# An fp32 hybrid encoder layer on one core: the lower half's x asked for together, the gate rows loaded into a sweep tile, and attention's pool and first product re-ordered

## The chip, the cores and the metric

The kernel runs on one core of one Trainium2 chip. The metric is the device time of one execution in microseconds; several executions are run and their median is given. One execution is also recorded by the hardware profiler, and everything said below of single instructions, waits and transfers comes from that record. The engines are PE (TensorE: matmuls, with PEld loading the stationary operand), DVE (VectorE), ACT (ScalarE), POOL (GpSimd) and SP (SyncE, which here only issues DMAs). "ACTq" and "SPq" are the instructions with which ACT and SP issue a DMA.

## The reference

One encoder layer in fp32, 2048 tokens by 1024 channels, batch 1. Cut to its skeleton:

```python
u = _rms_norm(h, norm_mix_g[l])
proj = u @ w_in[l]
hy = _short_conv_centred(proj[..., :HY_COLS], hy_conv_w[l], hy_conv_b[l])
y_hy = _group_rms_norm(_hyena(hy, spec, hy_skip[l]), hy_norm_g[l], HYENA_GROUPS)
qk = jax.nn.silu(_short_conv_centred(proj[..., HY_COLS:off], ml_conv_w[l], ml_conv_b[l]))
y_ml = _mlstm_bidirectional(q, k, v, o, gates, ml_gate_b[l])
y_ml = _group_rms_norm(y_ml, ml_norm_g[l], MLSTM_HEADS)
h = h + jnp.concatenate([y_hy, y_ml], -1) @ w_out[l]
h = h + _cross_attention(_rms_norm(h, norm_x_g[l]), _rms_norm(mem, norm_mem_g[l]), wq, wk, wv, wo)
h = h + jnp.square(jax.nn.relu(_rms_norm(h, norm_ff_g[l]) @ ff_w1[l])) @ ff_w2[l]
return _rms_norm(h, final_norm_g)
```

The hyena is a long convolution of order two (two gated stages over all 2048 tokens, through a Fourier transform), the mLSTM is a gated linear recurrence in two directions over 4 heads of 128 channels, and the cross-attention looks at 256 memory tokens.

## The kernel before

**Arithmetic.** A full-precision product of two fp32 operands is made of three fp32r matmuls (`mm3`, lines 357, 360, 361): each operand is split by ACT into a rounded high part (a cast, L368) and by DVE into the rest (a subtraction, L368), and high x high, high x low and low x high are added in PSUM. The products of the memory projection (L679, L696, L708) use plain fp32 operands.

**Stages**, in the order in which `program` (L2019) weaves them:

1. The input projection, with x transposed: channels on partitions, tokens along the row. Only one half of the tokens (1024) fits on the chip at a time as `xh`/`xl`, so the projection runs over the upper half, then the lower (`hf` = 1, then 0). `sweep` makes columns that need the short convolution; `natural` makes v, o and gate columns with tokens on partitions, in tiles of 128 tokens x 256 or 272 columns (8 x 3 matmuls each), and ACT copies each tile out of PSUM (L859) and issues its store (`od<-st`, L860).
2. While the rest of the projection runs, the hyena's first and second stages (`hyena`) are woven in; they read and write `fs`, `zs`, `zg` and `hy` in DRAM through SP's and ACT's queues.
3. `memproj` (L664): eight heads' worth of keys and values of the memory, folded with `wq` and `wo`. Each product's result is copied to a small tile by ACT (`kt`, L681; `o`, L686), and ACT issues the store (`gd<-o`, L698; `vw<-o`, L710). The hyena's last stage and the first pieces of `mlstm` run beside it.
4. `attention` (L1381) over four blocks of 512 tokens, woven with the remaining chunks of `mlstm`: the mixed rows are turned by PE (L1423), multiplied by `w_out`, the residual is added, and scores, softmax and values follow.
5. The feed-forward stage (`ffn`), from about 1800 us to the end, a two-level recursive block product.

**What sets the order.** Python generators yield rough costs and `weave` interleaves two of them by those costs; a scheduler then orders the instructions of each engine by a simulated timeline, within the dependences. Each engine runs its own list strictly in order. Tiles come from pools with a tag and a number of buffers; a new tile of a tag waits until the oldest holder of that tag is read out. A pool that opens where another has closed waits in the same way for the last users of the addresses. Each DMA, on SP's queue or ACT's, also counts on one of eight semaphore lanes, and before it is issued waits for the previous DMA of its lane; so a store that ACT issues can be held by a load that SP issued long before.

**The x of a half.** `prep_x` (L639) chains two `x_chunk`s (L524) of four steps. A step takes a tile of 128 x 2 x 512 (512 KB) from DRAM by `x_load` (L517), scales its two halves by gain and by the rows' inverse norm on DVE (L510), casts it on ACT and subtracts on DVE (L368), and so fills a quarter of `xh`/`xl`. The tiles have the tag `xn` with two buffers, so a load goes out only when the step before last has been read. For the lower half this begins at step `t == 4` of the last tile row of `natural(1, (3, 0, 1, 2), ...)`; the products that need it follow directly in `natural(0, (3,))`. The sweeps use big tiles `P` and `cv` (128 x 1088, two each), which lie empty between the upper half's last sweep and the lower half's first.

**The gate rows.** `mlstm` (L1189) first loads the packed gate rows (`rows`, 8 DMAs of 32 x 512, 64 KB each, L1218) into two tiles of its own pool. For every chunk of 128 tokens `loads` spreads rows of these over 128 partitions on DVE (L1240), POOL adds a mask (L1256) and multiplies by q (L1255), ACT takes exponentials (L1258), DVE multiplies with the scores (L1259). After that a chunk's body is 16 matmuls with v and the state (L1287, L1289), then the normalisation (L1292 to L1303), and a state update (`update`, L1150: scaling by ACT, L1156, matmuls L1162, DVE L1168 into `cf`). A chunk loads q, k, v, the gate o, k again and the backward state: `qn`, `kk_t`, `va`, `og`, `kn`, `cbn`, about 256 KB each. Chunks 0 and 1 are loaded and chunk 0 is scored ahead of the loop. `take(m, 6)` runs six steps of `mlstm` beside `memproj`.

**The opening of attention.** `tail_open` (L1331) opens the pool T; its tags `wn` (4 staging tiles), `act` (4 tiles), `wh`/`wl` and `acc` get their addresses in the order in which they are first used. `mixed(0)` loads four tiles of the hyena's rows `yh`, turns them (L1423) and yields; then `stream` loads the first columns of `w_out`, and the first product is made in two halves: for its two column tiles the k range 0 to 3 (the hyena's half), which needs only `yh`, and then, when the mLSTM's rows `ym` of the first 512 tokens are there (`next(mix)`), the range 4 to 7.

## Time and profile before

| | |
|---|---|
| median of 3 executions | 3120.02 us (3117.74 to 3126.49) |
| the profiled execution, its own time | 3121.71 us |
| its span, from the first instruction to the last | 3120.0 us |
| its mean granted TensorE clock | 0.988 |
| DMA traffic | 607 MB, 195 GB/s on the mean |

A window row gives, for each engine, busy time and the number of instructions in a stretch, then the TensorE clock granted as a share of full speed, the share of the 16 DMA engines' time that was busy (summed over overlapping packets, so it can pass 1), and GB/s. In a row of waits, "A <- B: total, times, longest" says that A stood idle because of B. In a row of the timeline, the start and length of a group of instructions come first, and what stands in brackets is the idle time of the engine just before it and what ended it.

### The profile page before, as it was taken

To read this page: it belongs to the slowest core of one execution; us is meant where nothing else is said; L and a number is where in the kernel's file an instruction comes from. 1 tells how busy PE (TensorE), PEld (TensorE's weight loads), DVE (VectorE), ACT (ScalarE), POOL (GpSimd) and SP (SyncE) were. 2 spreads that over 40 slices of the span, in tenths; PEclk is the share of its full clock that TensorE was granted. 3 is DMA by queue.
4 is the path that set the end of the run, shared out by engine and by line. 5 is a ranking of instruction groups with operands and counts; after the bars stand their busy time and mean duration, and the time that the engine had idled before them with its cause. 6 is when DMAs were issued, how large, how long until landed. Compare 5 with 4: busy or idle time off the path is not lost.

```text
span 3120.0 us, 42912 instructions
## 1 busy us (share of the span) xinstructions
PE 3025.7 (97%) x14257; PEld 2374.8 (76%) x14257; DVE 1957.9 (63%) x3428; ACT 1498.4 (48%) x2930; POOL 1145.9 (37%) x802
## 2 busy tenths in 40 slices
PE   8999999989999898999999999999999999999998
PEld 6655667766677666888888888887888888888876
DVE  7865465446747356777665656657555686565696
ACT  6543465533646225555544455556455443333335
POOL 0122011200223243233142337766455475242693
PEclk9999999999999998999999999999999999999999
DMA  6554767676877996455375657656644565353434
GB/s 212 189 197 163 231 211 219 177 237 199 252 209 241 277 321 228 140 197 179 130 268 191 212 168 240 202 180 227 202 152 151 169 216 183 112 166 113 161 92 172
DMA packets 444102, 607.07 MB, mean 195 GB/s; under 512 B 38494, under 2 KB 248542, under 8 KB 442856
## 3 DMA queue, kind: packets, MB, share of 16 engines
q1 hardware_dynamic: 405988, 546.54, 54.3%
q10 hardware_dynamic: 37892, 57.79, 5.4%
q8 instruction: 113, 1.85, 0.2%
q14 instruction: 109, 0.89, 0.1%
HBM read 401.79 MB, written 202.41 MB: 194 GB/s over the span
## 4 chain that ended last, share of the span: by engine, by line
PE 55%; DVE 2%; issue 1%; DMA 1%; ACT 0%; POOL 0%; SPq 0%; ACTq 0%; POOLq 0%; DVEq 0%
PE mm L357 12%; PE mm L360 12%; PE mm L361 12%; PE hy L361 6%; PE hy L357 6%; PE hy L360 6%; DVE bl L1631 1%; PE hy L1287 1%; PE hy L1289 1%; DVE acc L1923 0%; PE hy L1534 0%; DVE acc L1957 0%; PE hy L1423 0%; DMA e<-hg 0%; PE hy L1249 0%
## 5 line engine op out<-in xcount | busy, mean ns | idle before, releaser
L1630 ACT CAST ah<-w 128x512 fp32r<-128x512 f32 x284 | 176.6, 622 | 304.8 <-PE hy L360 157.8
L1631 DVE TENSOR_TENSOR bl<-wr,bh 128x512 fp32r<-128x512 f32 x213 | 242.2, 1143 | 124.8 <-ACT bh L1630 124.2
L368 DVE TENSOR_TENSOR wl<-wn,wh 128x512 fp32r<-128x512 f32 (+1 forms) x300 | 220.6, 781 | 100.1 <-ACT wh L368 99.5
L998 POOL TENSOR_TENSOR b<-b,a 128x512 f32<-128x512 f32 x64 | 87.2, 1365 | 514.5 <-ACT b L996 215.4
L357 PE MATMUL mm<-xh,wh 128*128 128x512 f32 x640 | 267.5, 419 | 8.6 <-ACT wh L368 8.0
L360 PE MATMUL mm<-xl,wh 128*128 128x512 f32 x640 | 253.8, 397 | 1.3 <-DVE xl L368 1.3
L361 PE MATMUL mm<-xh,wl 128*128 128x512 f32 x640 | 255.0, 399 | 0.0
L1630 ACT CAST bh<-wr 128x512 fp32r<-128x512 f32 x232 | 143.5, 621 | 230.3 <-PE mm L361 173.1
L1631 DVE TENSOR_TENSOR al<-w,ah 128x512 fp32r<-128x512 f32 x236 | 216.8, 919 | 56.1 <-ACT ah L1630 56.0
L361 PE MATMUL mm<-bh,al 128*128 128x512 f32 x576 | 223.7, 391 | 2.6 <-POOL al L1631 2.6
L357 PE MATMUL mm<-bh,ah 128*128 128x512 f32 x576 | 225.6, 392 | 0.1
L360 PE MATMUL mm<-bl,ah 128*128 128x512 f32 x576 | 225.1, 391 | 0.0
L368 ACT CAST wh<-wn 128x512 fp32r<-128x512 f32 (+1 forms) x300 | 166.6, 618 | 113.9 <-PE mm L361 51.8
L360 PE MATMUL mm<-act,wh 128*128 128x512 f32 x512 | 200.6, 392 | 0.8 <-DVE act L368 0.8
L357 PE MATMUL mm<-act,wh 128*128 128x512 f32 x512 | 198.9, 394 | 1.4 <-ACT wh L368 1.3
L361 PE MATMUL mm<-act,wl 128*128 128x512 f32 x512 | 199.0, 392 | 0.0
L357 PE MATMUL hy<-bh,ah 128*128 128x512 f32 x448 | 175.2, 391 | 0.0
L360 PE MATMUL hy<-bl,ah 128*128 128x512 f32 x448 | 174.6, 390 | 0.0
L361 PE MATMUL hy<-bh,al 128*128 128x512 f32 x448 | 174.4, 390 | 0.0
L357 PEld LDWEIGHTS mm<-xh,wh 128*128 128x128 f32 x640 | 121.2, 190 | 60.9 <-issue 18.6
L357 PE MATMUL mm<-wh,xh 128*128 128x256 f32 (+1 forms) x512 | 155.2, 304 | 12.6 <-ACT xh L368 10.2
L361 PEld LDWEIGHTS mm<-xh,wl 128*128 128x128 f32 x640 | 121.0, 189 | 47.9 <-issue 23.2
(371 smaller groups left out, 8217.9 us busy)
## 6 DMA issues: line engine op xcount, KB each, us to landing
wr<-hc SPq DMA_DIRECT2D x224, 256.0 KB
w<-in_ff_w_dram SPq DMA_DIRECT2D x172, 256.0 KB
hc<-wn SPq DMA_DIRECT2D x128, 256.0 KB
wn<-in_w_in_dram SPq DMA_DIRECT2D x100, 256.0 KB
hc<-q SPq DMA_DIRECT2D x96, 256.0 KB
fs<-a SPq DMA_DIRECT2D x32, 512.0 KB
a<-fs SPq DMA_DIRECT2D x64, 256.0 KB
a<-zs SPq DMA_DIRECT2D x64, 256.0 KB
```

The costliest lines, as they stand in the source:

```text
L357: first = mm(ps, lh, rh, start=start, stop=False)
L360: mm(ps, lh, rl, start=False, stop=False)
L361: self.last = mm(ps, ll, rh, start=False, stop=stop)
L368: both = (self.nc.scalar.copy(hi, src), self.nc.vector.tensor_tensor(lo, src, hi.bitcast(F32), ALU.subtract))
L998: nc.gpsimd.tensor_tensor(xt, xt, hi[:, m], ALU.mult)
L1287: nc.tensor.matmul(dst, nm[:, h], va[:, h], start=True, stop=state is None)
L1289: nc.tensor.matmul(dst, rows_[d, 1][:, h], state[:, h], start=False, stop=True)
L1630: self.nc.scalar.copy(hi, src)
L1631: eng.tensor_tensor(lo, src, hi.bitcast(F32), ALU.subtract)
```

## The change

It has three parts.

1. **The lower half's x.** `x_chunks(hf)` replaces the two `x_chunk`s. For the lower half six of the eight loads are asked for together: the first two and no others in `xn` tiles, the next four in the four sweep tiles `P` and `cv`. This is called at `t == 0` of the last tile row of the upper half; the steps still start at `t == 4`. Loads seven and eight go out after steps one and two.
2. **The gate rows.** The eight loads move out of `mlstm` into `prep_mem`, into a `cv` tile (`rp`). In `mlstm` one DVE copy and one ACT copy take them to the two row tiles. One step of `mlstm` fewer is taken beside `memproj` (5 instead of 6); the weave with attention has 112 in place of 96.
3. **Attention.** T's addresses are given out in another order (`acc`, two `act` tiles, `wh`/`wl`, then the rest); `act` is split in two tags of two. The first columns of `w_out` are staged in tiles of attention's own pool ("we" loads), asked for before the first `yield`. The first half product (k 0 to 3) is made for four column tiles instead of two: the two of the first `w` and the two of the next (`self.peek`), with one more yield before the `ym` half.

```diff
-    def x_chunk(self, c):
...
-        xs = [self.x_load(c, 0)]
-        for j in range(4):
-            if j < 3:
-                xs.append(self.x_load(c, j + 1))
...
+    def x_chunks(self, hf):
+        parts = [(2 * hf + i, j) for i in range(2) for j in range(4)]
+        deep = 2 if hf else 6
+
+        def room(n):
+            if not 1 < n < deep:
+                return None
+            t = self.isb.tile([128, 1088], F32, tag=("P", "cv")[n % 2], name="xt", bufs=2)
+            return t[:, 0:D].rearrange("p (k t) -> p k t", k=2)
+
+        xs = [self.x_load(*parts[n], room(n)) for n in range(deep)]
+
+        def steps():
...
+                self.scaled(xs.pop(0), 2 * j, self.g_mix, rb, *(t[(slice(None),) + to] for t in (self.xh, self.xl)))
+                if n + deep < 8:
+                    xs.append(self.x_load(*parts[n + deep]))
+                yield
+        return steps()
...
         def halves():
             xs = [load(h) for h in range(2)]
+            by_half = self.dram("rows", (2, 128, 128)).rearrange("i (d s n h) t -> s (i d) n (h t)", d=2, s=2, n=8)
+            t = sb.tile([128, 1088], F32, tag="cv", name="rp", bufs=2)[:, 0:D]
+            self.early_rows = t.rearrange("p (s c) -> p s c", s=2)
+            for s in range(2):
+                for q in range(4):
+                    self.nc.sync.dma_start(out=self.early_rows[32 * q:32 * q + 32, s], in_=by_half[s])
...
+                    if after is True and t == 0:
+                        nxt = self.x_chunks(0)
+                    if t == at:
+                        if after is True:
+                            self.prepq = nxt
...
             t = sb.tile([128, 512], F32, name=f"rows{s}")
-            for q in range(4):
-                nc.sync.dma_start(out=t[32 * q:32 * q + 32], in_=by_half[s])
+            (nc.vector.tensor_copy if s == 0 else nc.scalar.copy)(t, self.early_rows[:, s])
...
-        self.T = es.enter_context(self.tc.tile_pool(name="t", bufs=1))
+        T = self.T = es.enter_context(self.tc.tile_pool(name="t", bufs=1))
+        self.acc = T.tile([128, 8, 512], F32, name="acc")
+        self.acts = 2
+        for _ in range(2):
+            self.act_tile("act")
+        for tag in ("wh", "wl"):
+            for _ in range(2):
+                T.tile([128, 8, 256], F32R, tag=tag, name=tag, bufs=2)
+        self.acts = 0
...
         def stream():
-            nxt = None
+            nxt = self.columns(items.pop(0), lambda: A.tile([128, 512], F32, tag="e", name="we", bufs=4))
             for w in items:
                 cur, nxt = nxt, self.columns(w)
-                if cur is not None:
-                    yield cur
+                self.peek = nxt
+                yield cur
             yield nxt
...
                     half = [gemm(w, i, y, None, range(4)) for i in range(2)]
+                    half += [gemm(self.peek, i, y, None, range(4)) for i in range(2)]
+                    yield 5.2
                     next(mix)
...
-                if c == 0 and ct < 2:
-                    p = gemm(w, ct, y, half[ct], range(4, 8))
+                if c == 0 and ct < 4:
+                    p = gemm(w, ct % 2, y, half[ct], range(4, 8))
...
-                rest = chain(s, p.sweep(range(4, 10), 1, True), p.natural(1, (3, 0, 1, 2), lambda: p.prep_x(0)),
+                rest = chain(s, p.sweep(range(4, 10), 1, True), p.natural(1, (3, 0, 1, 2), True),
...
-                             p.turned_in(), take(n, 2), beside_each(n, take(m, 6)))
+                             p.turned_in(), take(n, 2), beside_each(n, take(m, 5)))
...
-                weave(g, m, 440, 96, True)
+                weave(g, m, 440, 112, True)
```

**How it moves SP's queue: x.** Below is SP's list before, from the first x load of the lower half beyond the two early ones (its line is L521). `zg` and `hy` are the second hyena stage's reads, `wn` the projection's weights.

```order
L521 DMA xt<-in_x_t_dram 128x2x512 x2
L935 DMA a<-zg_2615 128x1024 x2
L938 DMA a<-hy 64x1024 x2
L935 DMA a<-zg_2615 128x1024 x2
L938 DMA a<-hy 64x1024 x2
L521 DMA xt<-in_x_t_dram 128x2x512
L935 DMA a<-zg_2615 128x1024 x2
L938 DMA a<-hy 64x1024 x2
L397 DMA wn<-in_w_in_dram 128x2x256 x2
L521 DMA xt<-in_x_t_dram 128x2x512
```

After the change four of these six stand far earlier, between the stores of the last upper sweeps (`kt<-cv`, `kn<-st`) and the reads of the hyena's first stage (`fs`, `zs`, with its tables `em` and `dm`). This piece has the first two of them; the next two stand two and eleven rows further on:

```order
L521 DMA xt<-in_x_t_dram 128x2x512
L831 DMA kt<-cv 128x1008
L397 DMA wn<-in_w_in_dram 128x2x256 x4
L936 DMA em<-in_c_em_dram 128x256
L927 DMA dm<-in_c_dm_dram 128x256
L931 DMA a<-fs_360 64x2x512 x2
L939 DMA a<-zs_2613 64x2x512 x2
L831 DMA kt<-cv 128x1008
L936 DMA em<-in_c_em_dram 128x256
L843 DMA kn<-st 128x4x128
L927 DMA dm<-in_c_dm_dram 128x256
L521 DMA xt<-in_x_t_dram 128x2x512
```

Four loads have thus moved from among the reads of `zg` and `hy` to among those of `fs` and `zs`; the last two stay among the `zg` reads.

**How it moves ACT's list: the first exponentials.** Before, at the start of `mlstm` beside `memproj` (`kt` and `o` are memproj's copies, `gd<-o` its store):

```order
L681 COPY kt<-mm 128x512
L213 ACTIVATE brm<-ms,eps 128x16
L681 COPY kt<-mm 128x512
L686 COPY o<-mm 128x512
L698 DMA gd<-o 128x2x256
L1258 ACT_TABLE_LOAD
L1258 ACTIVATE rw<-rw,cols 128x128 x4
L686 COPY o<-mm 128x512
L1258 ACTIVATE rw<-rw,cols 128x128 x6
```

After (L1241 is the copy of the second half of the rows, L1281 the exponentials, L701 the copy of `kt`, L706 that of `o`, L718 the store, L1182 the scaling of v):

```order
L1241 COPY rows_9571<-rp 128x512
L1281 ACT_TABLE_LOAD
L1281 ACTIVATE rw<-rw,cols 128x128 x16
L701 COPY kt<-mm 128x512
L213 ACTIVATE brm<-ms,eps 128x16
L701 COPY kt<-mm 128x512
L1182 ACTIVATE ve<-va,cols 128x129
L706 COPY o<-mm 128x512
L1182 ACTIVATE ve<-va,cols 128x129 x3
L718 DMA gd<-o 128x2x256
```

All sixteen exponentials of chunk 0 now stand ahead of memproj's first copies, and no longer behind its first store.

**How it moves PE's list and SP's queue: the opening of attention.** On PE before, from the end of the second chunk body after memproj's last product to the first product of attention (L357, L360):

```order
L1287 MATMUL hy<-va,rw 128x129
L1289 MATMUL hy<-cf,rw 128x129
L1287 MATMUL hy<-va,rw 128x129
L1289 MATMUL hy<-cbn,rw 128x129
L1287 MATMUL hy<-va,rw 128x129
L1289 MATMUL hy<-cbn,rw 128x129
L357 MATMUL mm<-act,wh 128x512
L360 MATMUL mm<-act,wh 128x512
```

After (L1188 is the update, L1458 the turn of `yh`, L1272 the scores, L1310 and L1312 the body):

```order
L1188 MATMUL hy<-ve,kn 128x129 x4
L1458 MATMUL hy<-ident,wn 128x128 x16
L1272 MATMUL hy<-qn,kk_t 128x128 x4
L1310 MATMUL hy<-va,rw 128x129
L1312 MATMUL hy<-cf,rw 128x129
L1310 MATMUL hy<-va,rw 128x129
L1312 MATMUL hy<-cf,rw 128x129
L357 MATMUL mm<-act,wh 128x512 x4
L1310 MATMUL hy<-va,rw 128x129
L1312 MATMUL hy<-cf,rw 128x129
```

What stands between memproj's last product and the turn of `yh` is of the same kinds and number in both (a chunk's scores, body and update); behind the turn the first product now comes after a quarter of the next body instead of three quarters, and further product matmuls stand between its later quarters. On SP's queue the first columns of `w_out` move as follows; before:

```order
L1417 DMA wn<-yh 128x512 x4
L1450 DMA acc<-in_x_t_dram 128x4x512 x2
L1140 DMA og<-od 128x512
L1224 DMA qn<-qt 128x4x128
L1224 DMA kk_t<-kt 128x4x128
L1323 DMA ym<-ht 128x512 x2
L1146 DMA va<-vd 128x4x128
L1224 DMA cbn<-cbd 128x516
L1140 DMA kn<-kn 128x512
L1348 DMA wn<-in_w_out_dram 128x2x256 x4
```

After:

```order
L1056 DMA yh<-a 64x1024 x2
L1383 DMA we<-in_w_out_dram 128x2x256 x2
L1247 DMA cbn<-cbd 128x516
L1172 DMA va<-vd 128x4x128
L1383 DMA we<-in_w_out_dram 128x2x256 x2
L1166 DMA kn<-kn 128x512
L1166 DMA og<-od 128x512
L1346 DMA ym<-ht 128x512 x2
L1247 DMA qn<-qt 128x4x128
```

The four loads now follow the hyena's last stores of `yh` directly and stand ahead of a chunk's `va`, `kn` and `og`; the load of `yh` itself comes later, nine rows further down the list.

More of the change, by code (lines that the diff above doesn't have):

```diff
@@ L844, in natural @@
                     yield 11
-                if t == at and c2 == tiles[-1] and after is not None:
-                    after()
+                if c2 == tiles[-1] and after is not None:
+                    if after is True and t == 0:
[3 more added lines that the diff above has]
+                            self.prepq = nxt
+                        else:
+                            after()
                 ts = slice(128 * t, 128 * t + 128)
@@ L1331, in tail_open, with act_tile, columns @@
     def tail_open(self, es):
-        self.T = es.enter_context(self.tc.tile_pool(name="t", bufs=1))
+        T = self.T = es.enter_context(self.tc.tile_pool(name="t", bufs=1))
[7 more added lines that the diff above has]
+        self.acts = 0
     def stage(self):
         return self.T.tile([128, 512], F32, tag="wn", name="wn", bufs=4)
+    def act_tile(self, name):
+        self.acts += 1
+        return self.T.tile([128, 8, 512], F32R, tag=f"act{(self.acts - 1) // 2 % 2}", name=name, bufs=2)
     def act(self):
-        return [self.T.tile([128, 8, 512], F32R, tag="act", name="act", bufs=4) for _ in range(2)]
-    def columns(self, w):
+        return [self.act_tile("act") for _ in range(2)]
+    def columns(self, w, stage=None):
         hi = self.T.tile([128, 8, 256], F32R, tag="wh", name="wh", bufs=2)
@@ L1444, in attention @@
         stats = None
[L1445 removed]
+        acc = self.acc
         for c in range(4):
@@ L1657, in ffn_x @@
         else:
-            x = T.tile([128, 8, 512], F32R, tag="act", name="x", bufs=4)
+            x = self.act_tile("x")
             hi, lo = x[:, 0:4], x[:, 4:8]
```

16 lines of the change are left out of this document (7 added, 9 removed).

## The prediction, made before the changed kernel was run

> **What bounds the kernel now.** I read the page's totals first, then all waits of PE, then the windows around the three places that the change touches.
>
> ```profile
> span 3120.0 us, 42912 instructions
> PE 3025.7 (97%) x14257; PEld 2374.8 (76%) x14257; DVE 1957.9 (63%) x3428; ACT 1498.4 (48%) x2930; POOL 1145.9 (37%) x802
> ```
>
> PE is busy for 3025.7 of 3120.0 us, so all idle time of PE together is 94 us. None of the three parts takes a matmul away, so what can be won is that idle time, and the slow clock that follows it. The list of PE's waits over the whole run says where it lies:
>
> ```profile
> PE mm L696 <- ACT o L686: 11.3, 2, 10.1
> PE mm L357 <- ACT xh L368: 10.2, 2, 7.4
> PE hy L1287 <- DVE bry L218: 7.4, 2, 5.7
> PE mm L679 <- ACT o L686: 5.0, 2, 4.4
> PE hy L1162 <- ACT ht L1301: 4.5, 1, 4.5
> PE hy L1423 <- DVE act L368: 1.5, 1, 1.5
> PE hy L1423 <- DVE cf L1168: 1.1, 1, 1.1
> ```
>
> Lines 1 and 4 are memproj, line 2 the lower half's x, the rest mLSTM and attention's opening. The windows (PE is the first figure behind the stretch's length; at the end stand PE's clock, the DMA share and GB/s) give the three places in turn: x of the lower half, memproj, attention's opening.
>
> ```profile
> 640.00:660.00 20.00, 18.58 (x124) 14.20 (x122) 10.78 (x17) 5.22 (x9) 0.00 (x0) 1.00 0.99 300
> 660.00:680.00 20.00, 12.88 (x72) 10.53 (x73) 9.24 (x14) 5.06 (x8) 0.00 (x0) 0.74 0.97 301
> 680.00:700.00 20.00, 17.28 (x87) 12.16 (x85) 7.92 (x14) 5.72 (x11) 0.00 (x0) 1.00 0.66 190
> 1040.00:1060.00 20.00, 20.00 (x93) 16.20 (x92) 11.52 (x36) 1.48 (x3) 7.64 (x6) 1.00 0.93 297
> 1060.00:1080.00 20.00, 9.23 (x28) 6.99 (x27) 3.57 (x14) 10.63 (x30) 7.34 (x6) 0.66 1.03 307
> 1080.00:1100.00 20.00, 19.29 (x86) 13.74 (x85) 8.93 (x22) 2.56 (x5) 8.08 (x6) 1.00 1.04 356
> 1100.00:1120.00 20.00, 14.48 (x60) 11.01 (x61) 7.16 (x19) 2.54 (x5) 3.98 (x4) 0.91 1.01 325
> 1120.00:1140.00 20.00, 18.26 (x101) 14.72 (x101) 13.16 (x43) 5.03 (x16) 10.41 (x8) 1.00 1.03 323
> 1200.00:1220.00 20.00, 10.51 (x60) 8.66 (x58) 12.15 (x51) 7.96 (x33) 7.13 (x7) 0.78 0.81 276
> 1220.00:1240.00 20.00, 17.05 (x96) 15.70 (x97) 14.61 (x32) 12.32 (x42) 9.53 (x7) 0.79 0.71 224
> 1240.00:1260.00 20.00, 17.41 (x93) 14.86 (x92) 14.90 (x47) 11.87 (x39) 4.24 (x4) 0.91 0.56 185
> ```
>
> PE's idle time is 1.4 + 7.1 + 2.7 = 11.3 us at x, 0 + 10.8 + 0.7 + 5.5 + 1.7 = 18.7 us at memproj, 9.5 + 3.0 + 2.6 = 15.0 us at attention's opening: 45 of the 94 us. Busy time at a low clock is a second loss, estimated as busy time times the missing clock: 12.88 x 0.26 = 3.3 us, 9.23 x 0.34 + 14.48 x 0.09 = 4.4 us, and 10.51 x 0.22 + 17.05 x 0.21 + 17.41 x 0.09 = 7.5 us. So the most that could be had is about 14.6, 23.1 and 22.5 us.
>
> **Part 1, the x.** These rows, from waits and timeline around 640 to 700 us, show what is late:
>
> ```profile
> DVE xt L510 <- DMA xt<-in_x_t_dram: 10.3, 3, 4.3
> ACT st L859 <- DMA a<-zg: 9.3, 1, 9.3
> 656.60 0.37 SPq L521 DMA_DIRECT2D xt<-in_x_t_dram  x1
> 664.93 1.04 ACT L368 CAST xh<-xt 128x1024 fp32r<-128x1024 f32 x1 [1.87 <-DMA wn<-in_w_in_dram]
> 666.02 0.59 PE L357 MATMUL mm<-wh,xh 128*128 128x272 f32 x1 [7.44 <-ACT xh L368]
> 680.86 1.42 DVE L510 SCALAR_TENSOR_TENSOR xt<-xt,par,rb 128x512 f32<-128x512 f32 x2 [2.78 <-DMA xt<-in_x_t_dram]
> ```
>
> PE waits twice, 7.4 us and 10.2 - 7.4 = 2.8 us. The short one is plain: DVE's scaling waited 2.78 us for the load of x. The long one has two parents. The cast at 664.93 stood in ACT's list behind a store of `od`, held 9.3 us by a `zg` load on its lane, and the x loads, 0.5 MB each, are in flight between those `zg` loads at a DMA share of 0.97 to 0.99. The change takes four loads out of that stretch, 2.1 MB, which at 300 GB/s are 7 us of DMA; and in the new order the third and fourth casts stand among ACT's first held stores rather than behind them all. I take the 10.2 us as gone but for 1.5 us, and two thirds of the clock loss: 8.7 + 2.2 = **11 us won**. Bounds: only the short wait goes, 2.8; everything goes, 14.6.
>
> What it costs is paid where the loads now stand. In the old run's time their new neighbours are issued between 487 and 512 us:
>
> ```profile
> 490.00:500.00 10.00, 8.66 (x41) 5.72 (x40) 9.19 (x14) 8.73 (x14) 4.26 (x3) 1.00 0.95 286
> 500.00:510.00 10.00, 9.88 (x51) 6.50 (x51) 7.61 (x13) 8.72 (x16) 3.50 (x3) 1.00 0.86 276
> ```
>
> The DMA engines are nearly full there too, and PE idles 1.46 us. 2.1 MB at 286 GB/s are 7.3 us. Behind each load on SP's queue stand the reads of the hyena's first stage, which PE needs. If all of it reached PE, 7.3 us are lost; if the natural tiles, which need none of these reads, cover it, nothing. As PE has such tiles between the hyena's pieces there I take **1.5 us lost**, as much again as its idle time now.
>
> **Part 2, the gate rows and a chunk less.**
>
> ```profile
> 1042.19 6.37 SPq L1218 DMA_DIRECT2D rows<-rows  x5
> ACT L1258 <- DMA qn<-qt: 20.6, 1, 20.6
> DVE rw L1240 <- DMA rows<-rows: 5.7, 1, 5.7
> 1068.45 0.38 ACTq L698 DMA_DIRECT2D gd<-o  x1
> 1071.95 6.71 PE L696 MATMUL mm<-kt,wm 128*128 128x256 f32 x16 [10.14 <-ACT o L686]
> 1079.29 3.72 PE L696 MATMUL mm<-kt,wm 128*128 128x256 f32 x16 [0.62 <-ACT kt L681]
> ```
>
> ACT's store of `gd` was held 20.6 us until the `qn` load on its lane had landed, and `qn` was issued behind the eight loads of rows. Behind that store stood the exponentials and the copies of `o`, for which PE waited 10.1 us; then its 16 matmuls took 6.71 instead of 3.72 us. Together that is 13.1 us, the most that this place gives: rows now come before the stage, and the exponentials stand ahead of the first store. The two copies of rows, 128 x 512 each, lie on DVE and ACT, which are 58% and 7% busy at 1040 to 1060, and cost nothing on PE's path; uncovered, the nearest copy of this size (ACT's `o`, 0.59 us, two of them) makes 1.2 us.
>
> But memproj moves bytes at a share of 0.93 to 1.04 for 100 us. If bytes alone set its length, the gain is the bytes that leave it: the rows, 8 x 64 KB, and one chunk, 6 x 256 KB, 2.1 MB in all, at 325 GB/s 6.5 us. A lane that is held moves on to another store rather than vanishing. Between 6.5 and 13.1 us I take **8 us won**, near the lower figure since the share is above 1. Below it the bounds reach to 0, when another lane holds ACT as long; the `o` waits of 4.4 us around 1108 have nothing to do with rows, and the chunk less may remove them (13.1 + 5.0 + their clock 1.3 = 19.4 at most). The chunk's matmuls are done in attention instead: moved, not saved.
>
> The Trainium skill's page DMA: Bandwidth & Descriptors says under "Issuing engines are not separate DMA queues" that transfers started by SP, ACT or POOL run on the same 16 engines, and under "Where 436 GB/s comes from" that HBM gives a core about 358 GB/s. By that figure the 32 MB of 1040 to 1140 us would need an estimated 90 us, 10 us less than they took, so bytes would leave room for the whole wait, and the term would be 13. The share in the rows, above 1 at 307 GB/s already, speaks against such room, and the sum goes by the rows.
>
> **Part 3, attention's opening.**
>
> ```profile
> 1213.53 0.77 PE L1287 MATMUL hy<-va,rw 128*128 128x129 f32 x2 [5.75 <-DVE bry L218]
> 1222.95 2.09 PE L1162 MATMUL hy<-ve,kn 128*128 128x129 f32 x8 [4.46 <-ACT ht L1301]
> 1238.19 0.39 PE L357 MATMUL mm<-act,wh 128*128 128x512 f32 x1
> 1238.42 0.39 PE L360 MATMUL mm<-act,wh 128*128 128x512 f32 x1
> ACT ve L1156 <- DMA va<-vd: 3.2, 1, 3.2
> ```
>
> A matmul of the first product starts every 0.23 us. A half product is 4 x 3 of these, 2.7 us; the change makes four before it needs `ym`, 10.9 us of work where 5.5 us stood, and puts them after a quarter of a chunk body. That covers the two waits at the turn of `ym`, 1.5 + 1.1 us, and their clock in 1240 to 1260 (1.6 us): 4.2 us. One more chunk of the mLSTM now lies among products; the total of PE's work is unchanged.
>
> The large waits, 5.75 and 4.46 us, come before any product in PE's list, and in the new list still do: the chunk's body and update stand ahead of the turn of `yh` as before. They are not won by order. Nor are they safe: ACT waited 3.2 us for `va` in this chain, and four loads of `w_out` (1 MB, at 276 GB/s 3.8 us) now go out ahead of a chunk's `va`. Bounds: 3.8 lost to 22.5 won. I take **4 us won**.
>
> **Sum.** -11 + 1.5 - 8 - 4 = -21.5 us. The profiled execution took 3121.7 us, 1.7 above the median, so it would take 3100.2, and the median is forecast at 3120.0 - 21.5 = **3098.5 us**.
>
> **Rivals.** 0.3% are 9.4 us, about what a measurement of this kernel tells from no change; so faster is below 3110.7, slower above 3129.4.
>
> *The waits of memproj only move.* For it: the DMA share above 1, and a lane wait needs only some slow load. Against: 2.1 MB leave. Then part 2 gives nothing: 3120.0 - 11 + 1.5 - 4 = 3106.5.
>
> *ACT's held store still holds the casts of x.* For it: the 9.3 us were a `zg` load's, and these stay. Against: the new order of casts. Then part 1 gives the short wait alone, 2.8: 3120.0 - 2.8 + 1.5 - 8 - 4 = 3106.7.
>
> *It doesn't do what it says*: both of these, and part 3 as well only trades its waits: 3120.0 - 2.8 + 1.5 = 3118.7.
>
> *All three waits go with their clock*: 10.2 + 3.3 = 13.5 at x, 13.1 + 5.0 = 18.1 at memproj, and 4.2 + 5.75 = 10 at the opening, if the exposed chunk's loads come sooner too: 3120.0 - 41.6 + 1.5 = 3080.
>
> *Slower: SP is held at the early x loads.* A load into a `P` or `cv` tile must wait until the sweep's last store out of that tile has landed, and SP, in order, then holds the hyena's reads behind it. Four loads, each held as long as the longest lane wait seen here (9.3 us), would make 37 us; PE has natural tiles to cover some, so it decides if more than about 32 us of hold reach PE (21.5 + 1.5 won otherwise, and 9.4 to pass the bound). Price: 3120.0 + 37 - 23 = 3134. Against it: the sweeps' tiles were last used shortly before, and their stores are short.
>
> **Chances.** Forecast 0.45, memproj's waits move 0.15, the casts stay held 0.12, all go 0.15, it doesn't do what it says 0.07, SP held 0.06. The likeliest has its own range of 3090 to 3107. The whole range, 3079 to 3118, leaves out half of the best case, the slower one and half of the empty one, together under 0.2. Faster: 0.45 + 0.15 + 0.12 + 0.15 less 0.05 for the two 3106 cases that fall short, 0.82; same 0.12; slower 0.06.
>
> **What would show it.** Part 1: in the list of PE's waits the `xh` line falls below 2 us, DVE's wait for `xt` vanishes at the lower half, and the clock there is 1.00; if instead a store of `od` still holds ACT for some 9 us, the second rival is right. Its price: PE's idle time where the four loads stand, 1.5 us now. Part 2: the exponentials of chunk 0 run before memproj's first copy, no `gd` store waits 20 us, the `o` waits sum to under 6 us; if the sum stays near 16 at other stores, the first rival is right. Part 3: the waits of the `ym` turn vanish, while the 5.7 and 4.5 us ahead of the first product stay. The forecast is wrong if the window sums there stay near 15 us at x and memproj, or if idle time of more than 5 us appears around 490 to 520 us.

## The result, and the profile after

The changed kernel takes 3108.34 us (median of 7 executions, 3104.10 to 3113.61) against 3120.02 us (7 executions, 3115.71 to 3126.49). The ratio is 0.9962, 95% interval 0.9953 to 0.9972: 11.9 us faster, between 8.7 and 14.7. The forecast was 21.5 us faster, so the sign held and the time lies in the whole range of 3079 to 3118, but little more than half of the gain came: the time is outside the 3090 to 3107 that the likeliest case had, and nearest to the first two rivals, 3106.5 and 3106.7.

PE's busy time is the same to half a microsecond (3025.7 before, 3025.3 in a span of 3108.4 after). That is partly chance: over the fourteen profiles of this case, all with the same 14257 matmuls, it lies between 3019.4 and 3031.7 us, so idle time alone is not the whole account. The rows of PE's waits after the change that bear on it (who waits, on whom, total, times, longest; rows of stages that the change doesn't touch are left out):

```profile
PE hy L1188 <- ACT ht L1324: 7.6, 1, 7.6
PE hy L1458 <- DMA wn<-yh: 4.4, 1, 4.4
PE hy L1458 <- DVE act L368: 4.3, 1, 4.3
PE mm L716 <- ACT o L706: 3.4, 2, 3.1
PE mm L716 <- ACT kt L701: 2.4, 1, 2.4
PE mm L357 <- ACT xh L368: 2.3, 1, 2.3
PE mm L699 <- ACT o L706: 2.0, 1, 2.0
```

The `xh` wait fell from 10.2 to 2.3 us and memproj's `o` waits from 16.3 to 5.4; its `kt` wait rose from 0.6 to 2.4. New at the top are two waits at the turns of `yh` (L1458), 4.3 us within the first block's and 4.4 us ahead of the second block's, and a longer one for `ht`. To see what each stage gave, the same four stretches of both kernels, before first and after second (PE's busy time behind the length; PE's clock, DMA share and GB/s last). The stretches hold the x of the lower half, memproj, attention's opening, and the first block's end with the second block's turn:

```profile
600.00:720.00 120.00, 108.74 (x630) 84.06 (x629) 56.11 (x93) 42.99 (x77) 6.51 (x5) 0.96 0.72 217
980.00:1160.00 180.00, 159.92 (x783) 121.37 (x782) 90.22 (x236) 59.86 (x134) 60.91 (x48) 0.95 0.91 290
1160.00:1280.00 120.00, 104.97 (x551) 84.78 (x550) 80.44 (x237) 66.08 (x220) 47.75 (x36) 0.91 0.66 216
1280.00:1400.00 120.00, 118.45 (x641) 100.67 (x641) 88.37 (x229) 66.39 (x190) 30.56 (x23) 1.00 0.50 166
```

```profile
600.00:720.00 120.00, 115.53 (x661) 88.50 (x660) 60.34 (x104) 45.43 (x80) 6.51 (x5) 0.97 0.70 214
980.00:1160.00 180.00, 167.28 (x796) 124.59 (x795) 88.71 (x230) 58.91 (x132) 62.62 (x49) 0.95 0.93 300
1160.00:1280.00 120.00, 105.83 (x566) 87.54 (x565) 87.48 (x243) 67.91 (x215) 48.17 (x36) 0.94 0.65 207
1280.00:1400.00 120.00, 115.60 (x636) 99.50 (x635) 89.60 (x245) 70.72 (x221) 35.93 (x28) 0.97 0.56 177
```

Length less PE's busy time is idle time: 11.3, 20.1, 15.0 and 1.6 us before; 4.5, 12.7, 14.2 and 4.4 us after. So x gave 6.8 us, memproj 7.4, the opening 0.9, and the second block took 2.9 back, together 12.2; all other idle time of the run together changed by about 1 us the other way. That account is of one execution of each, and the windows are fixed in time while the changed kernel runs up to 11 us ahead, so a window doesn't hold quite the same work; the experiments show how far it may be trusted.

Where the four moved x loads now stand, the same windows that the prediction showed:

```profile
490.00:500.00 10.00, 8.66 (x41) 5.58 (x40) 8.48 (x13) 8.75 (x14) 5.20 (x3) 1.00 0.85 268
500.00:510.00 10.00, 9.88 (x56) 7.10 (x55) 7.46 (x12) 7.36 (x13) 2.56 (x2) 1.00 0.94 294
```

PE's idle time there is 1.34 + 0.12 us, to the hundredth what it was. The moved loads cost PE nothing there.

At the lower half's x, ACT's timeline after the change and PE's one wait there:

```profile
649.22 1.05 ACT L368 CAST xh<-xt 128x1024 fp32r<-128x1024 f32 x1 [4.10 <-DMA a<-hy]
655.01 1.05 ACT L368 CAST xh<-xt 128x1024 fp32r<-128x1024 f32 x1 [3.52 <-DMA a<-hy]
662.04 1.04 ACT L368 CAST xh<-xt 128x1024 fp32r<-128x1024 f32 x1 [5.70 <-DMA a<-hy]
663.14 0.39 PE L357 MATMUL mm<-wh,xh 128*128 128x272 f32 x1 [2.29 <-ACT xh L368]
```

DVE no longer waits for `xt`. What is left is ACT, held three times (13.3 us) at a store of `od` whose lane a load of `hy` has: the second rival's mechanism, at a smaller price for PE.

In memproj, the exponentials of chunk 0 run at once and ahead of the first copies, as the new order has it, but later stores are held:

```profile
1030.76 4.99 ACT L1281 ACTIVATE rw<-rw,cols 128x128 f32<-128x128 f32 x16 [0.86 <-POOL rw L1279]
1057.30 0.59 ACT L706 COPY o<-mm 128x512 f32<-128x512 f32 x1 [6.90 <-DMA kn<-kn]
1072.75 0.59 ACT L706 COPY o<-mm 128x512 f32<-128x512 f32 x1 [7.62 <-DMA wm<-in_xa_wq_t_dram]
1105.24 0.59 ACT L706 COPY o<-mm 128x512 f32<-128x512 f32 x1 [10.07 <-DMA wm<-in_xa_wo_dram]
```

The one hold of 20.6 us became several of 7 to 10 us at other loads. And at the second block of attention a wait stands that was not there (the window, then PE, ACT and SP in turn):

```profile
1320.00:1340.00 20.00, 15.60 (x85) 13.20 (x84) 17.99 (x48) 13.90 (x49) 6.36 (x5) 0.84 0.57 177
...
1335.85 2.10 PE L1458 MATMUL hy<-ident,wn 128*128 128x128 f32 x8 [4.40 <-DMA wn<-yh]
...
1331.51 2.16 ACT L368 CAST wh<-wn 128x512 fp32r<-128x512 f32 x4
...
1332.87 2.13 SPq L1452 DMA_DIRECT2D wn<-yh  x4
```

### The profile page after: what moved, and what is told of

Same layout as the page of the kernel before. It is cut to its first block, busy times and chain, and to the rows that moved or that the text cites. A ratio compares the mean times of both kernels' runs of the same rounds, so it can differ in the third digit from the quotient of the medians.

```text
span 3108.4 us, 42926 instructions
## 1 busy us (share of the span) xinstructions
PE 3025.3 (97%) x14257; PEld 2374.5 (76%) x14257; DVE 1955.3 (63%) x3429; ACT 1497.7 (48%) x2931; POOL 1141.1 (37%) x802
## 4 chain that ended last, share of the span: by engine, by line
PE 55%; DVE 3%; DMA 1%; issue 1%; ACT 1%; POOL 0%; SPq 0%; DVEq 0%; POOLq 0%; ACTq 0%
PE mm L361 12%; PE mm L357 12%; PE mm L360 12%; PE hy L357 6%; PE hy L361 6%; PE hy L360 6%; DVE bl L1668 1%; PE hy L1310 1%; PE hy L1312 1%; DVE acc L1960 0%; PE hy L1458 0%; DVE acc L1994 0%; PE hy L1571 0%; DMA va<-vd 0%; PE hy L1272 0%
## 5 line engine op out<-in xcount | busy, mean ns | idle before, releaser
L368 DVE TENSOR_TENSOR wl<-wn,wh 128x512 fp32r<-128x512 f32 (+1 forms) x296 | 213.1, 765 | 101.0 <-ACT wh L368 100.4
L357 PE MATMUL mm<-xh,wh 128*128 128x512 f32 x640 | 267.5, 419 | 8.5 <-ACT wh L368 7.9
L360 PE MATMUL mm<-xl,wh 128*128 128x512 f32 x640 | 253.7, 397 | 1.3 <-DVE xl L368 1.3
L357 PE MATMUL mm<-bh,ah 128*128 128x512 f32 x576 | 225.2, 391 | 1.8 <-DVE acc L1830 1.7
L360 PE MATMUL mm<-bl,ah 128*128 128x512 f32 x576 | 224.4, 390 | 0.0
L360 PE MATMUL mm<-act,wh 128*128 128x512 f32 x512 | 202.3, 395 | 0.0
L357 PE MATMUL mm<-act,wh 128*128 128x512 f32 x512 | 199.6, 396 | 1.3 <-ACT wh L368 1.2
L357 PE MATMUL hy<-bh,ah 128*128 128x512 f32 x448 | 175.2, 391 | 0.0
L360 PE MATMUL hy<-bl,ah 128*128 128x512 f32 x448 | 174.6, 390 | 0.0
L357 PEld LDWEIGHTS mm<-xh,wh 128*128 128x128 f32 x640 | 121.1, 189 | 60.8 <-issue 18.6
L357 PE MATMUL mm<-wh,xh 128*128 128x256 f32 (+1 forms) x512 | 156.0, 305 | 3.8 <-ACT xh L368 2.3
```

Of the source, the lines that this page charges most:

```text
L357: first = mm(ps, lh, rh, start=start, stop=False)
L360: mm(ps, lh, rl, start=False, stop=False)
L368: both = (self.nc.scalar.copy(hi, src), self.nc.vector.tensor_tensor(lo, src, hi.bitcast(F32), ALU.subtract))
```

## The experiments

**Each part alone.** Four kernels, each the kernel before with one part of the change. The edits are the pieces of the diff shown above; the moved chunk is

```diff
-                             p.turned_in(), take(n, 2), beside_each(n, take(m, 6)))
+                             p.turned_in(), take(n, 2), beside_each(n, take(m, 5)))
-                weave(g, m, 440, 96, True)
+                weave(g, m, 440, 112, True)
```

> The kernel before with the first part alone: six of the lower half's x loads asked for together. Theory A (the x wait is mostly gone, and what is left is ACT's stores of od held by loads of hy): PE's idle time between 600 and 720 us falls from 11.3 to about 4.5 us, clock 0.83 in 660 to 680, nothing new around 490 to 520 us, 3112 to 3114 us. Theory B (the part gave the 11 us that the prediction asked of it, and the other parts lost some): idle under 1.5 us there and 3109 us. Theory C (the moved loads cost what they win): within 2 us of 3120.

> The kernel before with the second part's loads alone: gate rows into a cv tile, six steps of the mLSTM beside memproj as before, weave 96. Theory A (the exponentials' place and the held gd store made the wait): the 10.1 us wait of L696 goes, 3 us are lost near 1000 us to the early row loads, where ACT's store of zg is held, net 5 to 8 us, 3112 to 3115 us. Theory B (memproj's length is set by bytes): the rows are 0.5 MB, at 325 GB/s 1.6 us, so 3118 us, with the same idle time at other stores.

> The kernel before with five instead of six steps of the mLSTM beside memproj and weave 112 in place of 96, nothing else. Theory A (held stores): the 10.1 us wait stays, the waits near 1108 us shrink, the second block's turn of yh waits about 4 us near 1325 us, net 3118 to 3122 us. Theory B (bytes): 1.6 MB less in memproj at 325 GB/s, 4.8 us, 3115 us, unless the new wait in attention takes it back.

> The kernel before with the third part alone: pool order, early columns of w_out, four half products. Theory A (the large waits stand ahead of the first product and stay): PE's idle time at 1200 to 1260 us falls from 15.0 to 11 to 14 us, 3116 to 3120 us. Theory B (the opening gains the 4 us of the prediction and more, and the chunk moved into attention took it back): idle under 10 us, 3112 to 3115 us. Theory C (the early columns delay the chunk's va): idle above 15 us, over 3121 us.

| kernel | ratio to before | 95% interval | us |
|---|---|---|---|
| x alone | 0.9973 | 0.9964 to 0.9983 | -8.4 |
| gate rows alone | 0.9999 | 0.9990 to 1.0008 | -0.3 |
| chunk and weave alone | 0.9987 | 0.9978 to 0.9997 | -4.1 |
| opening alone | 0.9986 | 0.9977 to 0.9995 | -4.4 |
| all (the change) | 0.9962 | 0.9953 to 0.9972 | -11.9 |

The last column is the ratio's distance from 1 times 3120. The parts add up to 17.2 us, the whole gives 11.9. But each interval is some 3 us wide to either side, and by the medians against the runs of before made with them the parts give 8.0, 0.7, 0.5 and 3.5 us, 12.7 together, against 11.7 for the whole. So it is not shown that the parts lose anything when they meet.

For x alone PE's waits between 600 and 720 us are only these two; idle there is 3.6 us:

```profile
PE hy L178 <- DVE a L1033: 1.9, 1, 1.9
PE mm L357 <- ACT xh L368: 1.6, 1, 1.6
```

Theory A of the x part holds: most of the stall gone, a rest with ACT; at 3111.12 us it is a microsecond faster than that theory's range. For the rows the long `o` wait goes as theory A has it (the longest left is 3.9 us) and idle in memproj is 16.4 us in place of 20.1 (first of the three rows below), yet the time, 3118.45 us, is that of theory B and of before. The chunk alone leaves memproj as it was, with 20.5 us idle, and wins in the opening, where idle falls from 15.0 to 10.1 us (second and third row):

```profile
980.00:1160.00 180.00, 163.62 (x784) 122.11 (x783) 87.55 (x222) 61.41 (x134) 59.67 (x48) 0.96 0.91 292
...
980.00:1160.00 180.00, 159.46 (x781) 121.36 (x780) 89.88 (x236) 60.45 (x134) 62.05 (x49) 0.95 0.91 291
1160.00:1280.00 120.00, 109.89 (x580) 87.89 (x579) 80.57 (x222) 65.93 (x203) 44.00 (x33) 0.96 0.68 217
```

The median, 3118.66 us, is in theory A's range and its 10 us wait stays, but both theories took the chunk to leave memproj, and nothing left it. The orders say why. On SP the kernels with six and with five steps have the same list up to some 25 rows behind memproj's last load of weights, and on PE up to the update that follows its last product. The scheduler had already put the sixth step's loads and matmuls behind memproj. The opening alone won in the opening (idle 12.8 us) and in the second block (0.4 us); its 3115.59 us lies just below theory A's range.

**Where the gain of the rows went.** Before and with the rows alone, PE has the same list of matmuls up to 1103 us, so the two can be compared instruction by instruction. At 988 us the kernel with the rows alone is 0.5 us behind; then come the early row loads, and memproj's first product starts at 1034.5 us against 1028.5. The windows at that place, before first:

```profile
1000.00:1020.00 20.00, 19.04 (x132) 16.39 (x131) 13.64 (x23) 12.37 (x20) 7.40 (x6) 1.00 0.68 211
1000.00:1020.00 20.00, 16.84 (x99) 12.69 (x98) 10.10 (x16) 11.19 (x17) 6.47 (x5) 0.91 0.70 215
```

In these 20 us PE gets 99 matmuls done in place of 132. ACT stands 3.0 us behind an `rp` load there, as theory A said, but DVE's list also has another order from 1008 us on; how the two share the price is not shown. The price stands in every kernel with the rows moved: with the x part, memproj's first product starts at 1019.4 us without the rows (x alone) and between 1023.0 and 1028.8 us with them, 1024.8 in the change. Memproj then wins 4 us of it back, the stall of 10 us being gone. But at the turn of `yh`, up to which both kernels have done the same matmuls, the rows alone stand at 1226.8 us and the kernel before at 1224.8. One thing more moved with the rows: between memproj's first and last product PE has 648 instructions in place of 696, and the 48 are one chunk's scores, body and update, which now stand behind memproj. So a chunk's matmuls did leave memproj, but by the rows and not by the step, and its loads did not.

**Is ACT held at stores the cause, or bytes?** Three kernels on top of the change. In the first two the stores are issued by POOL, in the third eight transfers are added:

```diff
-                nc.scalar.dma_start(out=(self.d_vd if c2 < 2 else self.d_od)[r0:r0 + 128, ...
+                nc.gpsimd.dma_start(out=(self.d_vd if c2 < 2 else self.d_od)[r0:r0 + 128, ...
```

```diff
-                nc.scalar.dma_start(out=gd[h // 2, :, 2 * i2:2 * i2 + 2, cs], in_=staged(p))
+                nc.gpsimd.dma_start(out=gd[h // 2, :, 2 * i2:2 * i2 + 2, cs], in_=staged(p))
...
-                    nc.scalar.dma_start(out=vw[2 * d:2 * d + 2, :, 2 * h + mt]...
+                    nc.gpsimd.dma_start(out=vw[2 * d:2 * d + 2, :, 2 * h + mt]...
```

```diff
+            self.extra = n = getattr(self, "extra", 0) + 1
+            self.behind(nc.sync.dma_start(out=self.dram("spare", (8, 128, 512))[n - 1],
+                                          in_=self.a["ff_w1"][0][0:128, 512 * n - 512:512 * n]))
```

> The changed kernel with the stores of the natural tiles (od and vd) issued by POOL instead of ACT. Theory A (what is left of the x stall is ACT held at these stores by loads of hy on their lanes, 4.1 + 3.5 + 5.7 us): the 2.3 us wait for xh and most of the rest goes, PE's idle time at 600 to 720 us falls from 4.5 to under 2 us, 3104 to 3107 us. Theory B (the stretch is short of DMA time, share 1.03): the casts come early but PE waits for other loads, idle stays 4 us or more, 3107 to 3111 us.

> The changed kernel with memproj's stores (gd and vw) issued by POOL instead of ACT. Theory A (held stores set memproj's stalls): the waits for o and kt, 7.8 us in the changed kernel, fall under 2 us, PE's idle time at 980 to 1160 us from 12.7 to about 6 us, 3101 to 3104 us. Theory B (bytes set it): the waits for o go but as much comes back at the loads of weights, keys or the hyena's reads, idle stays at 11 to 13 us, 3107 to 3110 us.

> The changed kernel with eight transfers of 256 KB from DRAM to DRAM added, one behind each project() of memproj on SP's queue, on which nothing waits: 2.1 MB more, as much as the change took out of the stage. Theory B (bytes set memproj's length): 6.5 us longer at 325 GB/s, 3114 to 3116 us. Theory A (held stores): the lanes move and the time stays within 3 us of 3108, or rises less than half as much.

*Stores of the natural tiles by POOL*: ratio to before 0.9953 (0.9940 to 0.9967), 3106.20 us. Its interval overlaps that of the change, so it isn't shown to be faster. The time is theory A's, the idle time between the two theories. The wait for `xh` is gone, but a wait in its place remains (PE's waits at 640 to 700 us):

```profile
PE mm L357 <- DVE sg L890: 2.8, 2, 2.6
PE hy L178 <- DMA a<-zg: 0.4, 1, 0.4
```

Idle at 600 to 720 us is 3.1 us against 4.5. With the stores on POOL the `xh` wait is gone in both kernels that have them so, and it stands in every other, which makes the held store its cause; the order of SP's list also changed a little, from 512 us on. What that is worth is not shown: the two kernels with POOL's stores have 3.1 and 4.1 us idle there, the others with the x part 3.6 to 4.5.

*memproj's stores by POOL*: 0.9983 (0.9974 to 0.9992), 3114.56 us, slower than the change. Theory A asked for 6 us of idle time in memproj; it is 11.2 (first row), as theory B has it, with 3.6 us of `o` and `kt` waits. The opening got worse, from 14.2 to 22.9 us (second row), and the time lies outside both theories:

```profile
980.00:1160.00 180.00, 168.76 (x800) 124.25 (x799) 85.12 (x225) 59.26 (x133) 78.05 (x72) 0.97 0.91 300
1160.00:1280.00 120.00, 97.12 (x527) 81.75 (x526) 81.78 (x228) 63.79 (x199) 50.09 (x41) 0.89 0.61 195
```

ACT now waits 15.7 us for `va` in memproj, where the change has 6.3:

```profile
ACT ve L1182 <- DMA va<-vd: 15.7, 2, 8.1
```

So held stores are not all that sets memproj's stalls; taken away, the next load is waited for. The edit also moved work: the scheduler ordered memproj anew, with 616 instructions of PE between its first and last product where the change has 648. How much of the opening's loss is that order and how much POOL's issuing is not shown.

*2.1 MB more*: 0.9969 (0.9958 to 0.9981), 3111.78 us. Idle in memproj rises to 20.1 us, but in the opening it falls to 9.3:

```profile
980.00:1160.00 180.00, 159.89 (x778) 122.69 (x777) 90.37 (x236) 57.26 (x134) 64.24 (x52) 0.93 0.94 301
1160.00:1280.00 120.00, 110.75 (x574) 88.36 (x573) 83.43 (x224) 66.94 (x203) 42.96 (x33) 0.96 0.69 216
```

That is 7.4 us more than in the change's profile, near the 6.5 that 325 GB/s says. But not bytes alone were added: the scheduler answered with another order, 712 instructions of PE between memproj's first and last product where the change has 648, and four more loads of a chunk on SP ahead of memproj's last weights. So a chunk's matmuls came back from the opening into memproj, which by itself would raise the one idle time and lower the other. Over the whole run the edit cost 2 to 3 us, which the intervals don't tell from none. It decides nothing between the two theories.

**Six steps beside memproj, all else as changed.** The two lines of the first diff of this section undone.

> The changed kernel with six steps of the mLSTM beside memproj and weave 96, as before the change; x, gate rows and opening as changed. Theory A (the chunk moved into attention takes back what the opening wins, 4.4 us at the second block's turn of yh): that wait goes and 3104 to 3107 us. Theory B (the chunk less is what relieves memproj): idle at 980 to 1160 us rises from 12.7 to 16 us or more, 3110 to 3113 us.

0.9971 (0.9960 to 0.9983), 3111.40 us: between the theories, and not told from the change. Both readings have a part: the wait at the second block is gone (idle at 1280 to 1400 us is 0.5 us, first row below, against 4.4), and the opening has 18.0 us idle instead of 14.2 (second row). In memproj idle is 16.6 us. As the instruction order of memproj is the same in both kernels, that 16.6 against 12.7 is no effect of the chunk; it is what one execution differs from another.

```profile
1280.00:1400.00 120.00, 119.46 (x657) 102.51 (x656) 92.60 (x244) 68.09 (x199) 36.74 (x28) 1.00 0.56 178
...
1160.00:1280.00 120.00, 102.00 (x534) 84.86 (x533) 85.81 (x241) 66.18 (x220) 47.60 (x36) 0.89 0.61 196
```

**One step fewer still, the second block's rows, and the early row loads.** On the changed kernel:

```diff
-beside_each(n, take(m, 5)))    weave(g, m, 440, 112, True)
+beside_each(n, take(m, 4)))    weave(g, m, 440, 128, True)
```

```diff
-            yn = self.stage()
+            yn = A.tile([128, 512], F32, tag="hg", name="yn", bufs=2) if r0 > 511 else self.stage()
```

```diff
-                    self.nc.sync.dma_start(out=self.early_rows[32 * q:32 * q + 32, s], in_=by_half[s])
+                    self.nc.gpsimd.dma_start(out=self.early_rows[32 * q:32 * q + 32, s], in_=by_half[s])
```

> The changed kernel with four steps of the mLSTM beside memproj and weave 128: another 1.6 MB and another chunk's matmuls go from memproj to attention. Theory B (bytes set memproj's stalls): PE's idle time at 980 to 1160 us falls from 12.7 to about 8 us; if attention covers the chunk, 3103 to 3105 us. Theory D (what memproj sheds, the opening or the second block pays in chains of the mLSTM): idle after 1160 us rises by as much, 3107 to 3112 us.

> The changed kernel with the rows yh and ym of blocks two to four staged in attention's hg tiles instead of the ring of four wn tiles that the weights use. Theory E (the new 4.4 us wait at 1335 us is the ring: the loads of yh wait until ACT has cast the weights, behind the exponentials of a chunk): the wait goes with its clock, 3101 to 3104 us. Theory F (it is PE's missing work, and the next thing, ym or the casts, ends last): as much idle time stays in 1280 to 1400 us, 3106 to 3110 us.

> The changed kernel with the early loads of the gate rows issued by POOL instead of SP. Theory A (the early loads cost 3 us near 1000 us because ACT's store of zg is held by one of them): PE's idle time at 1000 to 1020 us falls from 3.1 to about 1 us, 3105 to 3107 us. Theory B (the share of the DMA engines there, not a lane): unchanged, 3107 to 3110 us.

> Stores of the natural tiles issued by POOL and the rows of blocks two to four staged in hg tiles, both on the changed kernel. If the two add: 3099 to 3102 us. If the second has no effect: 3105 to 3107 us.

*Four steps*: 1.0008 (0.9999 to 1.0017), 3125.95 us; the whole gain is gone, and the time is 14 us above theory D's range. Memproj's idle time, 16.8 us, did not fall, against theory B. PE's waits at 1160 to 1420 us, and the longest of them:

```profile
PE hy L1458 <- DMA wn<-ym: 13.6, 4, 10.3
PE hy L1458 <- DVE wl L368: 6.2, 1, 6.2
PE hy L1458 <- DVE act L368: 1.1, 1, 1.1
```

```profile
1228.72 1.09 PE L1458 MATMUL hy<-ident,wn 128*128 128x128 f32 x4 [10.31 <-DMA wn<-ym]
```

Four chunks of the mLSTM must be done before the turn of the first 512 tokens' `ym`. With a step fewer ahead, the four half products, 10.9 us of PE, no longer bridge it. This is theory D's mechanism, at a larger price: a second chunk fewer can't be covered. That the third part of the change is needed to cover the first is not shown: the chunk alone, without the third part, waits only 2.3 us for `ym`.

*Rows in hg tiles*: 1.0001 (0.9992 to 1.0010), 3122.24 us; 12 us worse than the change by the ratios, and far outside both theories. There are only two such tiles in place of four, and turns now wait all through the later blocks; the rows below are PE's waits from 1280 to 1860 us. The wait for `yh` went, as theory E has it, and others came in greater number; idle at 1280 to 1400 us is 6.6 us. As the edit changed the number of tiles too, it decides nothing on the ring; whether four further tiles would win the 4.4 us was not tried.

```profile
PE hy L1458 <- DMA yn<-ym: 9.0, 5, 2.4
PE hy L1458 <- DVE act L368: 4.3, 2, 3.8
```

*Row loads by POOL*: 0.9961 (0.9947 to 0.9974), 3109.49 us, the time of the change. At 1000 to 1020 us, idle falls from 3.1 to 1.3 us:

```profile
1000.00:1020.00 20.00, 18.74 (x113) 15.31 (x114) 10.40 (x25) 8.06 (x15) 6.07 (x5) 0.91 0.40 132
```

Theory A has the place right, but the time is theory B's. The loads still delay memproj: its first product starts at 1023.0 us, 1.7 us sooner than in the change but 3.6 us later than with x alone. This kernel has 19.5 us idle at 980 to 1160 us and 10.6 us in the opening, in an order of its own from 991 us on, and still the time of the change: idle time in one stage says little of the end. *Both POOL stores and hg tiles*: 0.9987 (0.9977 to 0.9998), 3118.67 us, outside both expectations: the hg tiles cost here too. No version is shown to beat the change; the one with POOL's stores is level with it.

**How far one profile goes.** Several of these kernels have the same instruction order within memproj. PE's idle time at 980 to 1160 us with the old order: 20.1 (before), 21.7 (x alone), 20.5 (chunk alone), 19.8 (opening alone), mean 20.5. With the new order: 12.7 (the change), 16.4 (rows alone), 16.6 (six steps), 16.8 (four steps), 17.1 (hg tiles), mean 15.9. So the new order is worth 4.6 us of idle time there and not the 7.4 that the change's own profile shows, and it comes with the rows alone. The other five kernels have orders of their own there, with 11.2 to 20.1 us. At x the same comparison gives 10.3 to 11.8 us without that part and 3.1 to 4.5 with it in all fourteen profiles; at the second block 4.3 to 4.8 in the five kernels that have all parts with five steps and rows in wn tiles, and 0.4 to 2.3 in those with another number of steps or without one of the parts.

## Why the prediction was right or wrong, point by point

**The x, 11 us: right mechanism, perhaps a little too large.** x alone measured 8.4 us (5.3 to 11.2), so 11 is at the edge. I allowed 1.5 us for a rest; idle of 3.6 to 4.5 us stayed, since ACT's stores are still held, now by `hy`. The clock at 660 to 680 rose from 0.74 to 0.83 only, and the `xh` line stayed at 2.3 us, not below 2. The second rival named this hold; it cost PE 2.3 us, not the 7.4 it was priced at.

**The price of the early loads, 1.5 us: nothing.** The idle time at 490 to 510 us is unchanged although the share rose to 1.02 at 510 to 520. The slower rival, SP held at those loads, had no part in it.

**The rows and a chunk less, 8 us: this is the step that failed.** It rested on "the bytes that leave it: the rows, 8 x 64 KB, and one chunk, 6 x 256 KB, 2.1 MB in all". The chunk's loads did not leave memproj: they were behind memproj's last loads already, as the order of SP's list shows. Of the 2.1 MB only the 0.5 MB of rows left, by my own rate 1.6 us. The hold of 20.6 us on ACT vanished as forecast, but other stores were held 7 to 10 us each, so of the 13.1 us at that place 4.6 us of idle time remain as gain over several executions. And the sum had no price for the row loads where they now stand, ahead of the stage, though it had one for the x loads: there PE fell 5.5 us back (from 0.5 us behind to 6.0), and only 4.0 us of it were won again by the turn of `yh`. That is why the 3.7 us less idle time of that profile did not show in the time; its PE is also busy 4.2 us longer (3029.9 against 3025.7). The rows alone gave 0.3 us (3.1 faster to 2.5 slower), the chunk alone 4.1 (0.9 to 6.9, by the medians 0.5), and that in the opening. The first rival, that the waits only move, is nearer to this than the forecast. The signs that I had named for this part all came (exponentials first, no hold of 20 us, `o` waits of 5.4 us together): they looked only inside the stage, and the price stood ahead of it.

The Trainium skill's figure under "Where 436 GB/s comes from" in DMA: Bandwidth & Descriptors would have made this term 13. In the change's profile one window of memproj moved more than its 358 GB/s and PE was not idle in it:

```profile
1080.00:1100.00 20.00, 20.00 (x95) 14.89 (x94) 10.52 (x31) 3.13 (x6) 5.69 (x5) 1.00 1.06 369
```

So the figure is no ceiling for a 20 us stretch of this mix, and the room that it leaves was not turned into time either.

**The opening, 4 us: the size was right, by luck.** Alone it gave 4.4 us (1.6 to 7.2). I said that the waits of 5.75 and 4.46 us ahead of the first product stay; in the change their kind stays (7.6 us for `ht`), and idle in the opening fell by 0.9 us in that profile. The waits at the turn of `ym`, 1.5 and 1.1 us, are gone as forecast, but 4.3 us within the first turn of `yh` came in their place. Why the part alone gave its 4.4 us was not shown.

**What the sum lacked besides: a look behind the last changed place.** The prediction placed nothing behind 1260 us. At the second block 4.3 to 4.8 us of idle time, a wait for `yh`, appear in all five kernels that have all parts, five steps and rows in wn tiles, and in no other; in the change's own profile that is 2.9 us more than before, with some 2 to 3 us of slow clock (15.6 us of PE at 0.84). The clock differs from kernel to kernel, from 0.84 to 1.00 in that window. Whether this is what the whole lacks against its parts stays open, since the lack of 5.3 us is itself not shown. Why SP issues those `yh` loads late was read from the order of the ring of tiles, not shown: the experiment that was to show it changed the number of tiles as well.

## What to carry to other kernels

When a generator's step is moved to another stage, compare the instruction lists and count only what crosses the border; a scheduler may have put the work behind the border long before, and an edit that adds or moves a few transfers may make it order a whole stage anew. A load that moves has a price at its new place as well: where two kernels have the same instruction list, compare the start of one and the same instruction on both sides of that place. Where all stages wait for each other in chains, a stall that is taken away is worth its idle time only up to the next wait: measure the parts alone, and look behind the changed stage for a wait that only the combination has. Before reading a few microseconds out of one profile, look at several executions of the same order.

## What the runs showed of the hardware that was not expected

The same instruction order gave memproj 12.7 to 17.1 us of PE idle time in five executions at a DMA share of 0.91 to 0.93 over the stretch, though the old order varied only from 19.8 to 21.7. The same 14257 matmuls kept PE busy for 3019.4 to 3031.7 us in fourteen profiles, at a mean granted clock of 0.987 to 0.992. Where eight loads of 64 KB, half a megabyte, were issued among the reads of another stage, PE fell 5.5 us back (rows alone, 988 to 1034 us). Stores issued by POOL instead of ACT ended ACT's holds at the x (the `xh` wait of 2.3 us gone); in memproj the same exchange made the run 6 us longer (3114.56 against 3108.34), with the loss in the stage behind it and in another instruction order, so that the cause is not shown.
